# Conditioning vectors as 2048-wide weighted sums, 8 KB weight slots and an opening in eight steps, in a two-layer decoder trunk

## The chip, the cores and the metric

The kernel runs on one core of a Trainium2 chip. The metric is the device time of one execution in microseconds (us), as the median of several runs. The parts of the core are called TensorE (PE in the profile, with PEld for its weight loads), VectorE (DVE), ScalarE (ACT), GpSimd (POOL) and SyncE (SP), which issues most of the DMAs.

## The reference

One sequence of 256 tokens with 2048 features passes through two decoder layers, all in float32. Layer 0 mixes tokens with forgetting attention (FoX, 16 heads of 128), layer 1 with sliding-window grouped attention (SWA, 32 query heads of 64, 4 key/value heads). Each layer then has a gated feed-forward network with a causal convolution (5632 wide). Around each of the four sub-layers stands the conditioning by a vector c:

```python
c_act = jax.nn.silu(c)                              # (1, 2048)
for i in range(DEPTH):                              # 2
    mod = c_act @ ada_w[i] + ada_b[i]               # 2048 x 12288 weights a layer
    sh1, sc1, g1, sh2, sc2, g2 = jnp.split(mod[:, None, :], 6, axis=-1)
    h = x * (1.0 + sc1) + sh1
    y = mixer(h)                                    # fox_attention or swa_attention
    x = layer_norm(DEEPNORM_ALPHA * x + (1.0 + g1) * y, ln_mix_g[i], ln_mix_b[i])
    h = x * (1.0 + sc2) + sh2
    y = conv_ffn(h, ffn_w_up[i], ffn_conv_w[i], ffn_conv_b[i], ffn_w_down[i])
    x = layer_norm(DEEPNORM_ALPHA * x + (1.0 + g2) * y, ln_ffn_g[i], ln_ffn_b[i])
return x
```

The conditioning weights `ada_w` hold 2 x 2048 x 12288 floats, 201 MB of the 600 MB that the kernel reads.

## The kernel before, in words

**Products.** Activations lie transposed in `hH` and `hL`, the rounded value and the remainder of each float, features on the partitions. Weights come in tiles of 128 x 1024 floats (512 KB: two row blocks of 128 by 512 columns) through a pool `wp` of 10 slots of 4 KB a partition. `stream` (L266) issues the DMA on SP, has ScalarE round the tile into `wh` (L272) and VectorE take the remainder into `wl` (L283); the products run two tiles later. Each product is the sum of three: hH by wh, hL by wh, hH by wl. With the weights stationary (`w_mm`, results `ws`) a tile takes 24 products of 256 columns; with the activations stationary (`x_mm`, results `xs`) 12 products of 512 columns. The hidden list `work` holds what is still to be emitted, so the order on every engine is written out by the program.

**Background work.** After each tile `tick` (L367) runs: it adds `ada["rate"]` to a debt and makes one step of the conditioning generator `ada_vector` (L381) for each whole unit. A step before is one DMA of 512 KB (128 rows of c by 1024 columns of `ada_w`) and one VectorE operation (L405) that adds the rows, scaled by the entry of c on their partition, to `acc`. 32 such steps make one of the ten vectors of 2048 that are made this way, `(layer, part)`, and `acc` must still be summed over the partitions: for shift and scale columns by 16 TensorE transposes and ScalarE sums (L469, L473, layer 0) or by VectorE transposes and sums (L447, L451) with a product by `fold` (layer 1); for gate rows (parts 2 and 5) by a split on ScalarE and VectorE and products with ones (the result in `gate`, L421). A gate's bias is put into `acc` by a GpSimd DMA (L393). Rates are set by stage (1.6 a tile at the start of FoX, 0.64 in the first feed-forward). `ada_need` runs the steps that are missing when a vector is wanted.

**Opening.** The first two vectors, shift and scale of layer 0, are needed before any product. `opening` (L565) makes them from `ada_open`, a copy of their weights in tiles of 512 KB, in five steps that cover 1, 1, 2, 2 and 2 pairs of feature blocks (`STEPS`). In a step VectorE adds up the rows (`oacc`, L605), TensorE multiplies some row blocks directly (`products`) and then sums `oacc` over the partitions (`totals`): these are products of one column, in the bank `cps`. Then `cv` (L644) is made, x is transposed (`mod_turn`, L526) and modulated into hH and hL (`mod_pair`, L540, L541). Between these, FoX tiles that need only finished feature blocks are streamed: `plan` lists the pairs (block of 512 columns, pair of feature blocks) by step, each three tiles (query, key, value). Results of a block that is not finished in the opening are copied aside by `keep` (L948) and added later (`sum`, L881).

**Placement.** `place` sets where hH and hL start inside the padded buffer `hpad`: 20 floats in for FoX and the feed-forwards, 56 in for SWA.

Of the kernel before, what the change touches and what calls it, by code (L numbers as in the profile page):

```python
# [17 lines left out]
P = 128  # L18
# [23 lines left out]
def hybrid_trunk(ctx: ExitStack, tc: tile.TileContext, a: dict, out: bass.AP):  # L42
# [13 lines left out]
    def wtile(name="w"):  # L56
        return wp.tile([P, 2, WB], F32, tag="w", name=name)
# [34 lines left out]
    rows0 = ttile("rows0").rearrange("p (a b) -> p a b", b=P)  # L92
    NADA = 6 * KC
    nc.sync.dma_start(rows0[:KC, 0, :], a["c"].rearrange("b (r p) -> (b r) p", p=P))
    adab = a["ada_b"].rearrange("l (r p) -> l r p", p=P)
    nc.sync.dma_start(rows0[:NADA, 1, :], adab[0])

    ones = cst.tile([P, P], F32, name="ones")
# [21 lines left out]
    csil = tp.tile([KC, P], F32, tag="t", name="csil")  # L120
    nc.scalar.activation(csil, rows0[:KC, 0, :], AF.Silu)
    cact = cst.tile([P, KC], F32, name="cact")
    pt = bank()
    nc.tensor.transpose(pt[:, :KC], csil, ident[:KC, :KC])
    nc.vector.tensor_copy(cact, pt[:, :KC])
    cactp = cst.tile([P, KC], F32, name="cactp")
    nc.gpsimd.tensor_scalar_mul(cactp, cact, float(P))
    acol = cst.tile([P, DEPTH, NADA], F32, name="acol")
    pt = bank()
    nc.tensor.transpose(pt[:, :NADA], rows0[:NADA, 1, :], ident[:NADA, :NADA])  # L130
    nc.vector.tensor_copy(acol[:, 0, :], pt[:, :NADA])
# [4 lines left out]
    fold = cst.tile([P, 4, P], F32, name="fold")  # L136
    nc.gpsimd.memset(fold, 0.0)

    NF = 2 * DFF // P
    HR = ROPE_DIM // 2  # L140
# [7 lines left out]
    def columns():  # L148

        r = ttile("rows").rearrange("p (a b) -> p a b", b=P)  # L150
        for l in range(1, DEPTH):
            nc.gpsimd.dma_start(r[:NADA, l, :], adab[l])
        for q, nm in enumerate(("ln_mix_g", "ln_mix_b", "ln_ffn_g", "ln_ffn_b")):
            nc.gpsimd.dma_start(r[q * 32:(q + 1) * 32, 0, :], a[nm].rearrange("l (r p) -> (l r) p", p=P))
        yield
        for l in range(1, DEPTH):
            pt = bank()
            nc.tensor.transpose(pt[:, :NADA], r[:NADA, l, :], ident[:NADA, :NADA])
            yield
            nc.vector.tensor_copy(acol[:, l, :], pt[:, :NADA])  # L160
        pt = bank()
        nc.tensor.transpose(pt[:, :P], r[:, 0, :], ident)
        yield
        nc.vector.tensor_copy(lcol.rearrange("p a b c -> p (a b c)"), pt[:, :P])
        for l in range(DEPTH):
            r = ttile("rows").rearrange("p (a b) -> p a b", b=P)
            for j in range(CW):
                nc.gpsimd.dma_start(r[:NF, j, :], a["ffn_conv_w"][l, j].rearrange("(r p) -> r p", p=P))
            nc.gpsimd.dma_start(r[:NF, CW, :], a["ffn_conv_b"][l].rearrange("(r p) -> r p", p=P))
            for _ in range(4):  # L170
                yield
            pt = bank()
            for j in range(CW + 1):
                nc.tensor.transpose(pt[:, j * NF:(j + 1) * NF], r[:NF, j, :], ident[:NF, :NF])
            yield
            nc.vector.tensor_copy(ccol[:, l].rearrange("p a b -> p (a b)"), pt[:, :(CW + 1) * NF])

    def rotary():

        nc.gpsimd.dma_start(sink, a["swa_sinks"][0].partition_broadcast(P))  # L180
        posr = tp.tile([NT, P], I32, tag="t", name="posr")
        nc.gpsimd.dma_start(posr, a["positions"].rearrange("b (t p) -> (b t) p", p=P))
        yield
        for q in range(4):
            nc.vector.tensor_reduce(fold[:, q, q * 32:(q + 1) * 32], ident.rearrange("p (a i) -> p i a", a=4),
                                    axis=AX.X, op=ALU.add)
        nc.vector.tensor_scalar_mul(nsink, sink, -1.0)
        posf = tp.tile([NT, P], F32, tag="t", name="posf")
        nc.vector.tensor_copy(posf, posr)
        yield  # L190
        pt = bank()
        nc.tensor.transpose(pt[:, :NT], posf, ident[:NT, :NT])
        yield
        posc = cst.tile([P, NT], F32, name="posc")
        nc.vector.tensor_copy(posc, pt[:, :NT])
# [69 lines left out]

    def stream(wsrc, row0, col, ks, use, spare={}):  # L266

        for kc in ks[::2]:
            w = wtile()
            pin(nc.sync.dma_start(w, wsrc[(row0 + kc) // 2, col // WB]), False)  # L270
# [22 lines left out]
    def x_mm(ps, kc, h, l, stat, last, first=0, ts=range(NT)):  # L293

        for t in ts:
            for i in range(2):
# [20 lines left out]
    def w_mm(ps, kc, h, l, last=KC - 1, first=0):  # L317

        for i in range(2):
# [58 lines left out]
    held = []  # L378
    HELD = {}

    def ada_vector(l, v):  # L381
        row = v % 3 == 2
        if (l, v) in HELD and HELD[l, v]:
            q = [cst.tile([P, 512], F32, tag=f"ha{i}", name="ha") for i in range(4)]
            part = lambda c, n: q[c // 512][:, c % 512:c % 512 + n]
            step_ = 512
        else:
            acc = cst.tile([P, D], F32, tag="acc", name="acc")
            part = lambda c, n: acc[:, c:c + n]
            step_ = D // 2  # L390
        if row:

            nc.gpsimd.dma_start(acc, a["ada_b"][l, v * D:(v + 1) * D].partition_broadcast(P))  # L393
            yield
            yield
        for k in range(KC):
            for c in range(0, D, D // 2):
                w = wtile("wa").rearrange("p a f -> p (a f)")
                pin(nc.sync.dma_start(w, a["ada_w"][l, k * P:(k + 1) * P, v * D + c:v * D + c + D // 2]), False)
                for o in range(0, D // 2, step_):  # L400
                    ac, wo = part(c + o, step_), w[:, o:o + step_]
                    if k == 0 and not row:
                        pin(nc.vector.tensor_scalar_mul(ac, wo, cact[:, 0:1]), True)
                    else:
                        pin(nc.vector.scalar_tensor_tensor(ac, wo, (cactp if row else cact)[:, k:k + 1], ac,  # L405
                                                           op0=ALU.mult, op1=ALU.add), True)
                yield
        if row:
            while not ada["gate_free"]:
                yield  # L410
# [11 lines left out]
            gates[l, v] = g  # L422
            return
        ps = []

        def sums():
            ps.append(bank())
            for k in range(KC):
# [53 lines left out]
    def release():  # L482

        for s_, _ in held:
            s_()
# [771 lines left out]
```

## Time and profile before

| What | Value |
|---|---|
| median of 3 runs | 2203.82 us (2203.8 to 2205.1) |
| the profiled execution | 2204.25 us |
| its span, first to last instruction | 2202.5 us |
| granted TensorE clock, mean | 0.995 |
| PE busy, DVE busy, ACT busy, POOL busy | 98%, 82%, 52%, 1% |
| bytes moved by DMA | 602.98 MB, mean 274 GB/s |

The profile is one execution traced by the hardware. Times are microseconds unless marked ns. A line L75 is line 75 of the kernel; since helpers record the products, most of TensorE's work has the line L75 and is told apart by its tiles, written out<-in. Rows of groups give the count, the busy time, the mean duration of one in ns, and after it the idle time of the engine before them with what ended it. Products overlap one another, so their mean duration is longer than their pace. The chain is the work that ended last, followed back from the end: each piece with its start and how long it set the end. Rows of stretches give the stretch, its length and the busy time of each engine with the count of instructions, then the granted TensorE clock, the mean busy share of the 16 DMA engines and the GB/s moved.

### The profile page before, as it was taken

To read this page: it belongs to the slowest core of one execution; us is meant where nothing else is said; L and a number is where in the kernel's file an instruction comes from. 1 tells how busy PE (TensorE), PEld (TensorE's weight loads), DVE (VectorE), ACT (ScalarE), POOL (GpSimd) and SP (SyncE) were. 2 spreads that over 40 slices of the span, in tenths; PEclk is the share of its full clock that TensorE was granted. 3 is DMA by queue.
4 is the path that set the end of the run, shared out by engine and by line. 5 is a ranking of instruction groups with operands and counts; after the bars stand their busy time and mean duration, and the time that the engine had idled before them with its cause. 6 is when DMAs were issued, how large, how long until landed. Compare 5 with 4: busy or idle time off the path is not lost.

```text
span 2202.5 us, 38162 instructions
## 1 busy us (share of the span) xinstructions
PE 2156.7 (98%) x14883; PEld 1968.9 (89%) x14883; DVE 1810.4 (82%) x2487; ACT 1139.3 (52%) x1713; POOL 19.9 (1%) x49
## 2 busy tenths in 40 slices
PE   6999999999999999999999999999999999999997
PEld 6999888789999888999987877789999988999986
DVE  7879999989988989888989888899888655666765
ACT  3435646465565533555534687555555533555541
POOL 0000000000000000000000000000000000000000
PEclk9999999999999999999999999999999999999999
DMA  9999998969968989879888756778878666665662
GB/s 376 376 365 349 357 353 300 326 240 331 348 227 304 329 299 360 278 270 328 307 284 313 236 184 218 257 262 299 282 262 271 186 194 196 192 193 194 194 198 112
DMA packets 166598, 602.98 MB, mean 274 GB/s; under 512 B 18758, under 2 KB 19592, under 8 KB 165904
## 3 DMA queue, kind: packets, MB, share of 16 engines
q1 hardware_dynamic: 165360, 595.85, 78.1%
q0 software_dynamic: 1056, 4.69, 0.7%
q8 instruction: 116, 1.90, 0.3%
q14 instruction: 66, 0.54, 0.1%
HBM read 598.37 MB, written 2.10 MB: 273 GB/s over the span
## 4 chain that ended last, share of the span: by engine, by line
PE 84%; DVE 10%; issue 3%; ACT 2%; DMA 1%; SPq 0%; POOL 0%; DVEq 0%; ACTq 0%; POOLq 0%
PE ws L75 47%; PE xs L75 33%; DVE wl L283 3%; DVE acc L405 3%; DMA wo<-in_ada_open_dram 1%; ACT wh L272 1%; PE cps L75 1%; PE sm L526 1%; PE S L75 1%; DMA w<-in_fox_w_in_dram 1%; PE o L75 1%; DVE pr L734 1%; DVE oacc L605 0%; PE sm L75 0%; PE T L765 0%
## 5 line engine op out<-in xcount | busy, mean ns | idle before, releaser
L272 ACT CAST wh<-w 128x1024 fp32r<-128x1024 f32 x724 | 761.2, 1053 | 788.1 <-PE ws L75 271.2
L75 PE MATMUL ws<-hH,wh 128*128 128x256 f32 x6656 | 1148.9, 277 | 4.4 <-ACT hH L84 1.9
L283 DVE TENSOR_TENSOR wl<-w,wh 128x1024 fp32r<-128x1024 f32 x724 | 882.4, 1221 | 299.7 <-ACT wh L272 288.6
L75 PEld LDWEIGHTS ws<-hH,wh 128*128 128x128 f32 x6656 | 1009.3, 189 | 8.5 <-ACT hH L84 2.1
L75 PE MATMUL ws<-hH,wl 128*128 128x256 f32 x3328 | 916.5, 277 | 4.6 <-DVE wl L283 4.5
L75 PEld LDWEIGHTS ws<-hH,wl 128*128 128x128 f32 x3328 | 626.1, 189 | 6.5 <-DVE wl L283 6.2
L75 PE MATMUL xs<-wh,gT 128*128 128x512 f32 x1376 | 425.3, 389 | 0.0
L75 PEld LDWEIGHTS xs<-wh,gT 128*128 128x128 f32 x1376 | 258.3, 188 | 53.7
L75 PE MATMUL xs<-wl,gT 128*128 128x512 f32 x688 | 267.7, 389 | 0.0
L75 PE MATMUL xs<-wh,hH 128*128 128x512 f32 x704 | 235.8, 402 | 0.0
L405 DVE SCALAR_TENSOR_TENSOR acc<-wa,cact,acc 128x1024 f32<-128x1024 f32 x180 | 228.0, 1278 | 0.0
L405 DVE SCALAR_TENSOR_TENSOR acc<-wa,cactp,acc 128x1024 f32<-128x1024 f32 x128 | 162.5, 1278 | 0.0
L75 PEld LDWEIGHTS xs<-wh,hH 128*128 128x128 f32 x704 | 131.7, 189 | 29.1 <-ACT hH L84 0.3
L75 PEld LDWEIGHTS xs<-wl,gT 128*128 128x128 f32 x688 | 129.1, 188 | 26.5
L75 PE MATMUL xs<-wl,hH 128*128 128x512 f32 x352 | 139.6, 397 | 2.3 <-DVE wl L283 2.3
L1121 ACT ACTIVATE u<-ws,ccol 128x256 f32<-128x256 f32 x176 | 96.8, 562 | 62.1 <-PE ws L75 44.6
L75 PE MATMUL xs<-wh,oT 128*128 128x512 f32 x384 | 125.6, 396 | 0.0
L1122 DVE SCALAR_TENSOR_TENSOR u<-ws,ccol,u 128x255 f32<-128x255 f32 x176 | 82.5, 477 | 13.7 <-ACT u L1121 13.3
L75 PEld LDWEIGHTS xs<-wh,oT 128*128 128x128 f32 x384 | 72.1, 188 | 15.1
L1124 DVE SCALAR_TENSOR_TENSOR u<-ws,ccol,u 128x254 f32<-128x254 f32 x176 | 83.1, 477 | 2.0
L75 PEld LDWEIGHTS xs<-wl,hH 128*128 128x128 f32 x352 | 66.6, 189 | 17.4 <-DVE wl L283 4.1
L75 PE MATMUL xs<-wl,oT 128*128 128x512 f32 x192 | 75.4, 393 | 3.1 <-DVE wl L283 3.1
(231 smaller groups left out, 1290.8 us busy)
## 6 DMA issues: line engine op xcount, KB each, us to landing
w<-in_ffn_w_up_dram SPq DMA_DIRECT2D x352, 512.0 KB, 4.6
wa<-in_ada_w_dram SPq DMA_DIRECT2D x320, 512.0 KB, 5.3
w<-in_ffn_w_down_dram SPq DMA_DIRECT2D x176, 512.0 KB, 4.4
w<-in_fox_w_in_dram SPq DMA_DIRECT2D x96, 512.0 KB, 6.0
wo<-in_ada_open_dram SPq DMA_DIRECT2D x64, 512.0 KB, 8.2
w<-in_swa_w_in_dram SPq DMA_DIRECT2D x40, 512.0 KB, 4.7
w<-in_fox_w_o_dram SPq DMA_DIRECT2D x32, 512.0 KB, 5.4
w<-in_swa_w_o_dram SPq DMA_DIRECT2D x32, 512.0 KB, 4.4
```

What stands on the lines that cost most here:

```text
L75: return nc.tensor.matmul(o, lhsT, rhs, start=start, stop=stop, **kw)
L272: pin(nc.scalar.copy(h, w), False)
L283: pin(nc.vector.tensor_tensor(l, w, f32(h), op=ALU.subtract), behind[0] > 0)
L405: pin(nc.vector.scalar_tensor_tensor(ac, wo, (cactp if row else cact)[:, k:k + 1], ac, op0=ALU.mult, op1=ALU.add), True)
L526: nc.tensor.transpose(o[:, t * P:(t + 1) * P], x[:, t, (k + j) * P:(k + j + 1) * P], ident)
L734: nc.vector.tensor_tensor_reduce(pr[:, b:e].rearrange("p (a k) -> p a k", k=P), S_ps[:, b:e].rearrange("p (a k) -> p a k", k=P), mk, -1.0, ...
L1121: nc.scalar.activation(u, pf, AF.Identity, bias=cw(CW, f), scale=cw(2, f))
L1122: nc.vector.scalar_tensor_tensor(u[:, 1:], pf[:, :S - 1], cw(1, f), u[:, 1:], op0=ALU.mult, op1=ALU.add)
L1124: nc.vector.scalar_tensor_tensor(u[:, 2:], pf[:, :S - 2], cw(0, f), u[:, 2:], op0=ALU.mult, op1=ALU.add)
```

## The change

- `ada_w` is laid out column by column: block (layer, part, k) holds 128 output columns on the partitions with their 2048 weights behind one another. c, passed through SiLU, is kept on all partitions (`cb`, one broadcast DMA of 1 MB and one ScalarE operation). `ada_column` is one DMA of 1 MB and one VectorE `tensor_tensor_reduce` over 2048 elements, which multiplies by `cb`, sums, and starts from the bias: it gives the finished 128 entries. No sum over partitions is left. 32 operations make the opening's two vectors and 160 the other ten.
- A gate row is made from its column: 32 small ScalarE products with the identity matrix make diagonal tiles (rounded value and remainder), which are multiplied by ones; each of these steps refunds half a unit of debt.
- Slots of `wp` become 8 KB a partition, 6 of them. `stream` loads four row blocks (1 MB) at once where it can, and else puts two halves into one slot. All rates are halved.
- The opening has eight steps of one pair of feature blocks each: four `ada_column`s, x, and tiles by a new `plan`. The products of one column are gone. The first step modulates each feature block alone (`mod_one`), and the first block's products are split so that the half that needs the first feature block runs first (`second`). `mod_pair` can make both halves on ScalarE (`on_act`).
- Biases, norm parameters, convolution weights and positions come already laid out as columns, so their transposes go. `place` takes 60 and 32. `ones` moves to a temporary tile, `gp` has 28 buffers for 30, `release` and the held sums go.

```diff
-    wp = ctx.enter_context(tc.tile_pool(name="wp", bufs=10))
+    wp = ctx.enter_context(tc.tile_pool(name="wp", bufs=6))
...
-    gp = ctx.enter_context(tc.tile_pool(name="gp", bufs=30))
+    gp = ctx.enter_context(tc.tile_pool(name="gp", bufs=28))
...
-        return wp.tile([P, 2, WB], F32, tag="w", name=name)
+        return wp.tile([P, UK, WB], F32, tag="w", name=name)
...
+    cb = cst.tile([P, D], F32, name="cb")
+    nc.sync.dma_start(cb, a["c"][0].partition_broadcast(P))
+    acol = cst.tile([P, DEPTH, NADA], F32, name="acol")
+    nc.gpsimd.dma_start(acol, a["ada_b"])
...
+    nc.scalar.activation(cb, cb, AF.Silu)
...
         for kc in ks[::2]:
-            w = wtile()
-            pin(nc.sync.dma_start(w, wsrc[(row0 + kc) // 2, col // WB]), False)
+            g = row0 + kc
+            src = wsrc[g // UK, col // WB]
+            if kc in pend:
+                w = pend[kc]
+            elif g % UK == 0 and kc + 2 in ks:
+                W = wtile()
+                pin(nc.sync.dma_start(W, src), False)
+                w, pend[kc + 2] = W[:, :2], W[:, 2:]
+            else:
+                if halves:
+                    w = halves.pop()
+                else:
+                    W = wtile()
+                    w = W[:, :2]
+                    halves.append(W[:, 2:])
+                pin(nc.sync.dma_start(w, src[:, g % UK:g % UK + 2]), False)
...
+    def ada_column(l, v, k, cv):
+        w = wtile("wa").rearrange("p a f -> p (a f)")
+        pin(nc.sync.dma_start(w, a["ada_w"][l, v * KC + k]), False)
+        return nc.vector.tensor_tensor_reduce(w, w, cb, 1.0, acol[:, l, v * KC + k:v * KC + k + 1],
+                                              ALU.mult, ALU.add, cv[:, k:k + 1])
 
     def ada_vector(l, v):
...
+        cv = cst.tile([P, KC], F32, tag=f"cv{v}", name="cv")
         for k in range(KC):
...
+            pin(ada_column(l, v, k, cv), True)
+            yield
+        if v % 3 < 2:
+            cols[l, v] = cv
+            ada["held"] = v == 4
             return
+        gh, gl = (sp.tile([P, KC], F32R, tag=n, bufs=1, name=n) for n in ("gh", "gl"))
+        split_v(gh, gl, cv)
+        while not ada["gate_free"]:
+            yield
...
+        for j in range(nd + 3):
+            if j > 2:
+                nc.scalar.copy(g[:, (j - 3) * WB:(j - 2) * WB], ps.pop(j - 3))
+            if 1 < j < nd + 2:
+                ps[j - 2] = bank()
+                for i, d in enumerate(diag.pop(j - 2)):
+                    mm(ps[j - 2], onesr, d, start=i == 0, stop=i == 1)
+            if j < nd:
+                diag[j] = [gtile(n).rearrange("p a b -> p (a b)") for n in ("dh", "dl")]
+                for d, c in zip(diag[j], (gh, gl)):
+                    for q in range(WB // P):
+                        k = j * (WB // P) + q
+                        nc.scalar.mul(d[:, q * P:(q + 1) * P], ident, f32(c)[:, k:k + 1])
+            ada["debt"] += 0.5
+            yield
+        gates[l, v] = g
...
-    place(20)
+    place(60)
...
+    def mod_one(G, B, k):
+        ps, t = bank()[:, :S], ttile()[:, :S]
+        for j in range(NT):
+            nc.tensor.transpose(ps[:, j * P:(j + 1) * P], x[:, j, k * P:(k + 1) * P], ident)
+        g, b = G[:, k:k + 1], B[:, k:k + 1]
+        nc.scalar.activation(hH[:, k, :], ps, AF.Identity, bias=b, scale=g)
+        nc.scalar.activation(t, ps, AF.Identity, bias=b, scale=g)
+        nc.vector.tensor_tensor(hL[:, k, :], t, f32(hH[:, k, :]), op=ALU.subtract)
...
         todos = [[(*it, part) for it in items for part in range(3)] for items in plan]
-        for s_, todo in enumerate(todos):
+        for s_ in range(KC // 2):
+            k0, todo = 2 * s_, todos[s_]
             n = len(todo)
...
+            for i in range(4):
+                ada_column(0, 1 - i % 2, k0 + i // 2, cols[0, 1 - i % 2])
+                if i == 1:
+                    c = slice(k0 * P, (k0 + 2) * P)
                     nc.sync.dma_start(x[:, :, c], a["x"][0][:, c].rearrange("(t p) d -> p t d", p=P))
...
+                while todo and n - len(todo) < (i + 1) * n // 4:
                     proj(*todo.pop(0))
...
+                if s_ == 0 and i > 0:
+                    if i < 3:
+                        proj(*todos[1].pop(0))
+                    if i % 2:
+                        mod_one(cols[0, 1], cols[0, 0], i // 2)
+            if s_ > 0:
+                for _ in range(min(2, len(todos[s_ + 1]))):
+                    proj(*todos[s_ + 1].pop(0))
+                mod_pair(cols[0, 1], cols[0, 0], k0, mod_turn(k0), False, True, True)
+        prep()
+        then(lambda: ada.update(rate=0.8))
+        for it in todos[KC // 2]:
+            proj(*it)
...
-        plan = [[], [(2, 0), (1, 0)], [(1, 1), (3, 0), (3, 1)], [(3, 2), (3, 3), (0, 0), (0, 1)],
-                [(0, 2), (0, 3), (0, 4), (0, 5)], [(0, 6), (0, 7)]]
+        plan = [[], [(2, 0), (1, 0)], [(1, 1)], [(1, 2), (3, 0), (3, 1)], [(3, 2), (3, 3)], [(3, 4), (0, 0), (0, 1)],
+                [(0, 2), (0, 3), (0, 4)], [(0, 5), (0, 6)], [(0, 7)]]
...
-        for blk, rate in zip((0, 2, 1, 3), (1.6, 1.6, 1.5, 1.4)):
+        for blk, rate in zip((0, 2, 1, 3), (0.8, 0.8, 0.75, 0.7)):
...
-        place(20 if v else 56)
+        place(60 if v else 32)
...
+    out["ada_w"] = a["ada_w"].transpose(0, 2, 1).reshape(DEPTH, 6 * KC, P, D)
+    out["ada_b"] = a["ada_b"].reshape(DEPTH, 6 * KC, P).transpose(2, 0, 1)
```

More of the change, by code (lines that the diff above doesn't have):

```diff
@@ L119, in hybrid_trunk @@
     x = cst.tile([P, NT, D], F32, name="x")
[L120 to L131, printed above, removed]
+    nc.scalar.activation(cb, cb, AF.Silu)
+    for v in (1, 4):
+        c1 = acol[:, :, v * KC:(v + 2) * KC]
+        nc.gpsimd.tensor_scalar_add(c1, c1, 1.0)
     onesr = cst.tile([P, P], F32R, name="onesr")
     nc.vector.tensor_copy(onesr, ones)
[L136 to L140, printed above, removed]
     lcol = cst.tile([P, 4, DEPTH, KC], F32, name="lcol")
@@ L161, in columns @@
[L161 to L176, printed above, removed]
+        nc.gpsimd.dma_start(lcol, a["ln_col"])
@@ L178, in rotary @@
+        nc.gpsimd.dma_start(ccol, a["conv_col"])
+        yield
     def rotary():
         nc.gpsimd.dma_start(sink, a["swa_sinks"][0].partition_broadcast(P))
[L181 to L193, printed above, removed]
+        posr = cst.tile([P, NT], I32, name="posr")
+        nc.gpsimd.dma_start(posr, a["positions"])
+        for _ in range(3):
+            yield
+        pin(nc.vector.tensor_scalar_mul(nsink, sink, -1.0))
         posc = cst.tile([P, NT], F32, name="posc")
-        nc.vector.tensor_copy(posc, pt[:, :NT])
+        pin(nc.vector.tensor_copy(posc, posr))
```

287 lines of the change are left out of this document (64 added, 223 removed).

## The prediction

> **What bounds the kernel now.** I read the page first, then stretches by stage, then the chain of each stage.
>
> ```profile
> span 2202.5 us, 38162 instructions
> PE 2156.7 (98%) x14883; PEld 1968.9 (89%) x14883; DVE 1810.4 (82%) x2487; ACT 1139.3 (52%) x1713; POOL 19.9 (1%) x49
> PE 84%; DVE 10%; issue 3%; ACT 2%; DMA 1%; SPq 0%; POOL 0%; DVEq 0%; ACTq 0%; POOLq 0%
> ...
> 0.00:20.00 20.00, 11.05 (x46) 9.97 (x46) 10.57 (x20) 6.80 (x11) 4.10 (x21) 1.00 0.89 317
> 20.00:60.00 40.00, 32.25 (x187) 29.89 (x187) 34.86 (x44) 17.44 (x24) 0.00 (x0) 0.87 1.03 409
> 60.00:160.00 100.00, 99.43 (x716) 93.12 (x715) 84.34 (x83) 40.97 (x49) 2.52 (x5) 0.97 0.97 368
> 203.00:367.00 164.00, 158.01 (x1102) 143.94 (x1101) 152.78 (x228) 98.11 (x209) 0.57 (x1) 1.00 0.93 337
> 500.00:1100.00 600.00, 599.33 (x4644) 574.01 (x4644) 537.73 (x661) 309.91 (x403) 0.59 (x1) 1.00 0.88 308
> 1200.00:1410.00 210.00, 206.61 (x1152) 160.57 (x1153) 175.32 (x426) 146.68 (x335) 0.55 (x1) 1.00 0.65 210
> ```
>
> TensorE ends last for 84% of the span. In the feed-forward (500 to 1100) only less TensorE work can gain anything. The room is in three places: the opening, where the DMA engines are full (0.89 to 1.03 of their time) and TensorE starts late; FoX from 203 to 367, where VectorE is busy 152.78 of 164 us; and SWA after 1200.
>
> Busy time doesn't tell useful products from others, so I count weight tiles. The first two rows give the products with results ws and xs up to 203 us; then come their pace in the chain, the one-column products of a step's end, and the start of the first ws:
>
> ```profile
> 0.00:203.00 203.00, 111.94 (x866) 109.17 (x867) 2.75 (x4) 9.34 (x16) 0.96 0.97 369
> 0.00:203.00 203.00, 47.46 (x180) 33.62 (x180) 0.00 (x0) 4.38 (x8) 0.96 0.97 369
> ...
> 84.51 5.52 PE ws L75 x48
> 98.38 2.83 PE xs L75 x12
> 74.52 3.46 PE cps L75 x32
> ...
> L75 PEld LDWEIGHTS ws<-hH,wh x6656: 186/188/335, 21.0 to 2081.6; 128*128 128x128 f32 x196
> ```
>
> 866/24 + 180/12 = 51 tiles are done at 203 us. A tile costs (2 x 2.76 + 2.83)/3 = 2.78 us, so they are 142 us of useful work, and 61 of the first 203 us are lost: 21 before the first product, the rest at step ends.
>
> **The change, part by part.** *One conditioning operation.* Two operations of 1024 become one of 2048.
>
> ```profile
> L405 DVE SCALAR_TENSOR_TENSOR acc<-wa,cact,acc 128x1024 f32<-128x1024 f32 x180 | 228.0, 1278 | 0.0
> L734 DVE CUSTOM_DVE_ANT_0 pr<-S,mask,nsink 128x256 f32<-128x256 f32 x32 | 15.4, 480 | 0.0
> L734 DVE CUSTOM_DVE_ANT_0 pr<-S,mask,nsink 128x128 f32<-128x128 f32 x32 | 11.0, 344 | 0.0
> L734 DVE DVE_READ_ACCUMULATOR2_ANT nm<- 128x1 f32 x96 | 8.0, 84 | 0.0
> ...
> 200.94 2.39 DVE acc L405 x2
> ```
>
> The pair costs 2.39 us. The nearest rows for the new operation are the masked minima of attention, also `tensor_tensor_reduce`: (480 - 344)/128 = 1.06 ns an element, so 2048 take 480 + 1792 x 1.06 = 2384 ns. Back to back, operations overlap by about 83 ns (1278 against 2.39/2), which gives 2.30 us, or 2.38 if the read of the accumulator (84 ns) adds. I take 2.34: as good as even. These minima read one source from PSUM; L405 reads two f32 sources from SBUF at full rate, but writes no accumulator. No row has both, so the upper bound is open; one at half rate would be 2 x 2.3 = 4.6 us.
>
> [...]
>
> *The opening.* What each step must bring, in order on SP's queue: four columns of 1.05 MB, x 0.26, tiles of 0.524 each by `plan` (two of a step are pulled ahead), and first `cb`, 1.05. I run them at the stretches' rates: 6.3 MB by 20 us, 22.7 by 60, then 0.368 MB/us. Each pair of blocks is modulated some 4.5 us after its step's bytes land:
>
> ```profile
> L540 ACT ACTIVATE t<-sm,B,G 128x256 f32<-128x256 f32 x18 | 9.8, 561 | 0.1
> L84 ACT CAST hH<-t 128x512 fp32r<-128x512 f32 x25 | 15.5, 620 | 12.5 <-DVE t L541 12.2
> L85 DVE TENSOR_TENSOR hH<-t,hH 128x512 fp32r<-128x512 f32 x25 | 17.1, 686 | 0.5 <-ACT hH L84 0.4
> ```
>
> (2.34 for the last column, two of 0.56, 0.62 and 0.69, less what passes while the step's last tiles land.) The steps end at 6.6, 14.2, 20.2, 29.4, 37.0, 46.2, 55.4 and 61.4 MB, so at 21, 39, 54, 78, 99, 124, 149 and 165 us, and the pairs are ready at 25, 43.7, 58.5, 82.7, 103.5, 128.5, 153.5 and 169.5. TensorE then goes: 6 tiles to 42 (the first half-products run from about 14, when `cb` and two columns, 3.2 MB, have landed by 10 and 2.34 and two of 0.56 us have passed, which saves 2.7; 3 us are put down for the half clock behind waits, since the granted clock was 0.87 in 20 to 60); 3 tiles to 52.5; waits for the third pair; 9 tiles to 84; 6 to 101; waits 2.5; 9 to 129; 9 to 154.5; 6 to 171.6; the last 3 to **180 us**. That includes 0.45 us of transposes a step. The one-column products (144, gone) are no part of it. So 51 tiles are done at 180 instead of 203: **-23 us**. Bounds: TensorE never waiting after the second pair gives 43.7 + 45 x 2.78 + 4 = 173 (-30); each of the seven later ends losing 3.5 us, the length of the group at 74.52, instead of the 10 us of waits above gives 194 (-9). DMA is the cover that keeps TensorE from more: it stays full until 165.
>
> *The rest of FoX.* 45 tiles remain either way. Before, 55 operations of 1024 ran in 203 to 367 (66.44 us, first row below). After, the rates summed over those tiles give 36.8 steps, and with the refunds some 32 columns: 32 x 2.34 = 75 us. Gone is one gate's split (4 x 0.69). VectorE must do 75 - 66.4 - 2.7 = 5.9 us more in the stage where it is busy 93%: **+6 us** (0 if TensorE hides it, +12 if a long operation delays `wl` each time).
>
> ```profile
> 203.00:367.00 164.00, 66.44 (x55) 1.00 0.93 337
> ...
> L85 DVE TENSOR_TENSOR al<-acc,ah 128x512 fp32r<-128x512 f32 x16 | 10.8, 686 | 0.3 <-ACT ah L84 0.3
> L447 DVE STREAM_TRANSPOSE acc<-acc 128x512 f32<-128x512 f32 x16 | 10.9, 698 | 0.1
> L451 DVE TENSOR_REDUCE red<-acc 128x32 f32<-128x1024 f32 x8 | 9.6, 1203 | 0.0
> L469 PE MATMUL sm<-ident,acc 128*128 128x128 f32 x32 | 4.5, 272 | 0.0
> L75 PE MATMUL sm<-red,fold 128*128 128x16 f32 x32 | 3.8, 253 | 0.0
> L748 ACT ACTIVATE pr<-pr,ss 128x128 f32<-128x128 f32 x16 | 6.4, 402 | 4.2 <-DVE ss L746 4.1
> ...
> 1199.90 1.32 issue
> 1201.23 0.02 POOLq L393
> ```
>
> *Gates on ScalarE.* 32 products of 128x128, at most 402 ns each (L748), 13 us a gate instead of 4 casts. FoX's gate falls into a few tiles around 360, where each `wh` queues behind eight of them; two tiles of lead cover 5.6 us: **+2** (0 to +6). The other three gates go out at a lower rate: 0.
>
> *Sums over partitions.* 32 transposes (4.5 us) and 32 `fold` products (3.8) leave TensorE; where it is the only bound (the feed-forward, three of four vectors) that counts: **-2** (0 to -8).
>
> *The norm before SWA.* The chain waits 1.32 us for GpSimd, whose queue holds the gate's bias DMA (L393): **-1.3**.
>
> *SWA.* A vector's transposes and sums, 4 x 0.70 + 2 x 1.20, and one split, 2.7, leave VectorE, which is busy 175 of 210 us: **-3** (0 to -8).
>
> *Slots, queue, place.* Six slots of 1 MB hold 6 MB where ten held 5; a column blocks its slot until VectorE is done, as before: 0 (a stall of SP's queue would show in the opening, bound above). For `place` I add up the tile sizes: hH stands 112 bytes behind the weights (mod 256) before and after, 0 in SWA: 0, with the pace as rival.
>
> **Sum:** -23 + 6 + 2 - 2 - 1.3 - 3 = -21.3. The profiled execution took 2204.25 us (0.4 above the median of the runs), so **2183 us**.
>
> **Rivals.** *Given back.* FoX ends when the queue has brought its bytes: 130 MB by 367 before (the stretches' rates times their lengths, with 15 in 160 to 203). After: tiles 50.3, 64 columns 67.1, x and cb 3.1, and the same 9 read ahead, 129.5. At the same mean rate the first two terms are 0 and the time is 2200. For it: 0.93 to 1.03 busy engines. Against: VectorE's 93%, and 409 GB/s once.
>
> *More.* Opening at its bound, VectorE no hindrance: -30 - 2 - 1.3 - 8 = 2163.
>
> *Slower: the sum runs at half rate*, 4.6 us. Opening: 4 x 4.6 + 6.4 tiles x 1.14 + 0.7 = 26 us a step against 22: +28. FoX: 32 x 2.2 = 70; out projection 17 x 2.2 = 37; feed-forward 64 x 2.2 less its 62 us of room, 79; SWA 30. About 2430 us. It decides from about 2.65 us on, where 21 us are spread over some 69 operations on the path. The minima's slope speaks against it, their PSUM source leaves it open. [...]
>
> *Slower: another pace of the products.* Paces differ with the operands' places:
>
> ```profile
> 1108.14 71.97 PE xs L75 x317
> 869.72 73.48 PE ws L75 x648
> ```
>
> 236 ns with hH at 112 bytes (98.38 above), 227 with gT at 0, 113.4 for ws. If my sum of sizes is off and ws pays the same 3.5%, 9984 products cost 40 us more: 2223.
>
> **How the numbers follow.** The forecast 0.50 (2172 to 2194), given back 0.18, more 0.13, half rate 0.08, another pace 0.04, a stall of the six slots 0.07. 2162 to 2206 leaves out the last three and a little below. A difference under 0.2% (4.4 us) can't be told from none here: faster takes the forecast, more and half of given back, and a little of the rest, 0.74; same 0.12; slower 0.14.
>
> **What would show it.** Right: 51 tiles near 180 us, first ws near 14; no cps; the new operation near 2.38 us; FoX's last value tiles near 350; the rest shifted by a constant, ws still 113 ns. Wrong: the new operation over 2.65 us; VectorE's `wl` releasing TensorE in the feed-forward; the opening's last column far behind 165 us.

## The result and the profile after

The changed kernel takes 2193.45 us against 2205.1 us for the kernel before on the same chip: ratio 0.9944 [0.9928, 0.9960]; by the medians 11.7 us less. One of its five runs, at 7584.84 us, lies far outside the other four (2191.84 to 2195.05) and is left out of the ratio. The forecast was 2183, 21 less: the direction held, and a little under half of the gain is missing. The time lies just inside the forecast's stretch of 2172 to 2194.

From the page of the changed kernel: span, engines and shares of the chain; then the rows of the new operation.

```profile
span 2193.0 us, 36104 instructions
PE 2133.5 (97%) x14662; PEld 1941.2 (89%) x14662; DVE 1763.9 (80%) x2410; ACT 1160.8 (53%) x1770; POOL 15.6 (1%) x35
PE 86%; DVE 8%; issue 2%; ACT 2%; DMA 2%; POOL 0%; DVEq 0%; SPq 0%; ACTq 0%; POOLq 0%
```
```profile
L355 DVE CUSTOM_DVE_ANT_0 wa<-wa,cb,acol 128x2048 f32<-128x2048 f32 x192 | 450.0, 2345 | 7.3 <-DMA wa<-in_ada_w_dram 6.8
L355 DVE DVE_READ_ACCUMULATOR2_ANT cv<- 128x1 f32 x192 | 15.9, 83 | 0.0
```

TensorE has lost 23 us of busy time and the span only 9.5: part of the saved work came back as waiting. Where, the windows by stage show (columns as before: busy time and instructions of PE, PEld, DVE, ACT, POOL, then granted clock, DMA share, GB/s), with the useful products of the opening last:

```profile
0.00:20.00 20.00, 4.38 (x16) 3.43 (x16) 9.13 (x9) 10.31 (x14) 9.83 (x25) 1.00 0.92 352
20.00:60.00 40.00, 33.62 (x180) 28.76 (x181) 36.03 (x32) 17.52 (x25) 0.00 (x0) 0.91 1.02 418
60.00:160.00 100.00, 100.00 (x729) 93.25 (x728) 85.64 (x78) 49.93 (x61) 0.00 (x0) 1.00 1.01 404
178.40:342.90 164.50, 152.73 (x1102) 140.63 (x1100) 154.04 (x222) 87.54 (x154) 0.57 (x2) 1.00 0.90 340
500.00:1100.00 600.00, 600.00 (x4640) 574.39 (x4639) 532.10 (x648) 316.88 (x430) 0.00 (x0) 1.00 0.85 317
```
```profile
0.00:178.40 178.40, 103.41 (x816) 101.03 (x817) 1.38 (x2) 7.99 (x15) 0.98 0.99 396
0.00:178.40 178.40, 55.81 (x204) 38.90 (x204) 0.00 (x0) 3.94 (x7) 0.98 0.99 396
```

The last two rows are the products into ws and xs: 816/24 + 204/12 = 51 tiles, done at 178.4 us, where the kernel before had the same number at 203. From 60 to 160 us TensorE doesn't wait at all. In the feed-forward it is busy all the time too, as it was before.

Counting weight tiles (6144 columns each) along the trace in the same way gives the time at which every stage ends, and so what each term of the prediction was worth. Each column is one profiled execution, and these two differ by 9.2 us at the end where the medians differ by 11.7. Nine kernels with the new opening, at the same place of hH, reach tile 51 between 177.0 and 179.2 us; from there on, kernels that don't differ up to a point reach it in the same time to within 0.6 us.

| up to | before, us | after, us | this stage, us | predicted |
|---|---|---|---|---|
| tile 51, end of the opening | 202.8 | 178.4 | -24.4 | -23 |
| tile 96, end of FoX's input projections | 361.4 | 342.9 | +5.9 | +6 |
| tile 100 | 374.7 | 370.7 | **+14.5** | **+2** (gates) |
| tile 128, end of FoX's output projection | 463.8 | 460.4 | +0.6 | 0 |
| first `u` of the feed-forward | 494.8 | 494.2 | +2.8 | 0 |
| last residual before SWA | 1198.1 | 1193.6 | -3.9 | -2 (sums) |
| last residual of SWA | 1461.3 | 1451.4 | -5.4 | -4.3 (norm, SWA) |
| last residual of all | 2190.9 | 2181.7 | +0.7 | 0 |

One stage, four tiles long, holds the miss. Its two rows, before and after:

```profile
361.40:374.70 13.30, 13.30 (x65) 11.15 (x64) 11.77 (x14) 7.38 (x12) 0.00 (x0) 1.00 0.87 293
```
```profile
342.90:370.70 27.80, 23.69 (x93) 17.37 (x92) 13.04 (x32) 26.66 (x75) 0.00 (x0) 0.82 0.38 135
```

ScalarE went from 7.38 of 13.3 us to 26.66 of 27.8, TensorE fell to the half clock (granted 0.50) from 353.2 to 363.4 us, 0.82 in the mean of the stage, and the DMA engines were busy for 0.38 of the time, since SP's queue waited for slots, 12.9 us of it for one `wl`. The chain of the changed kernel there:

```profile
345.86 0.94 ACT wh L246
346.80 0.70 ACT pr L605 x2
347.50 1.17 ACT dh L387 x4
348.67 1.17 ACT dl L387 x4
349.85 1.17 ACT dh L387 x4
351.02 1.17 ACT dl L387 x4
352.18 0.36 ACT pT L624
352.55 0.89 ACT pr L595 x4
353.44 0.94 ACT wh L246
```

Two kinds of work stand between one cast of weights (`wh`) and the next: the gate's products (dh, dl, the change's own), and the softmax of attention (pr, pT), which in the kernel before was over by then.

### The profile page after: what moved, and what is told of

Its sections match the earlier page's. It is cut to its first block, busy times and chain, and to the rows that moved or that the text cites. A ratio compares the mean times of both kernels' runs of the same rounds, so it can differ in the third digit from the quotient of the medians.

```text
span 2193.0 us, 36104 instructions
## 1 busy us (share of the span) xinstructions
PE 2133.5 (97%) x14662; PEld 1941.2 (89%) x14662; DVE 1763.9 (80%) x2410; ACT 1160.8 (53%) x1770; POOL 15.6 (1%) x35
## 2 busy tenths in 40 slices
DMA packets 89671, 599.65 MB, mean 273 GB/s; under 512 B 10016, under 2 KB 12224, under 8 KB 21024
## 4 chain that ended last, share of the span: by engine, by line
PE 86%; DVE 8%; issue 2%; ACT 2%; DMA 2%; POOL 0%; DVEq 0%; SPq 0%; ACTq 0%; POOLq 0%
PE ws L75 48%; PE xs L75 34%; DVE wa L355 3%; DVE wl L257 2%; DMA wa<-in_ada_w_dram 1%; PE o L75 1%; PE S L75 1%; PE T L622 1%; DMA w<-in_fox_w_in_dram 1%; PE sm L428 1%; ACT wh L246 0%; DVE x L521 0%; DVE t L519 0%; PE sm L75 0%; PE spin L75 0%
## 5 line engine op out<-in xcount | busy, mean ns | idle before, releaser
L355 DVE CUSTOM_DVE_ANT_0 wa<-wa,cb,acol 128x2048 f32<-128x2048 f32 x192 | 450.0, 2345 | 7.3 <-DMA wa<-in_ada_w_dram 6.8
L75 PEld LDWEIGHTS xs<-wh,hH 128*128 128x128 f32 x704 | 133.0, 191 | 33.8 <-ACT wh L246 4.7
L595 ACT ACTIVATE pr<-pr,nm 128x128 f32<-128x128 f32 x96 | 43.1, 451 | 21.9 <-DVE nm L591 21.6
```

The costliest lines, as they stand in the source:

```text
L75: return nc.tensor.matmul(o, lhsT, rhs, start=start, stop=stop, **kw)
L355: return nc.vector.tensor_tensor_reduce(w, w, cb, 1.0, acol[:, l, v * KC + k:v * KC + k + 1], ALU.mult, ALU.add, cv[:, k:k + 1])
L595: nc.scalar.activation(pr[:, b:e], pr[:, b:e], AF.Exp, bias=nm[:, r:r + 1], scale=-1.0, accum_out=ss[:, r:r + 1])
```

## Experiments

### The gate's products: moved, doubled, paced

`gate_dve` and `gate_pool` make the same 32 products as eight operations of 128x512 on VectorE or GpSimd; `gate_twice` makes them twice for layer 0's first gate; `gate_norefund` drops the refund that makes the conditioning sums go on faster while a gate is made.

```
-    for q in range(WB // P):
-        k = j * (WB // P) + q
-        nc.scalar.mul(d[:, q * P:(q + 1) * P], ident, f32(c)[:, k:k + 1])
+    nc.vector.tensor_tensor(d (p, q, f), ident broadcast over q, c broadcast over f, op=ALU.mult)   # gate_dve
+    nc.gpsimd.tensor_tensor(... the same ...)                                                       # gate_pool
```
```
+    if (l, v) == (0, 2): nc.scalar.mul(...)      # gate_twice: the same product once more
...
-    ada["debt"] += 0.5                            # gate_norefund
```

> The 32 diagonal products of each gate go from ScalarE to VectorE, as 8 products of 128x512, some 0.6 us each, 4.8 us a gate. Theory (ScalarE burst): ScalarE is freed of 9.5 us in the chain, VectorE gets 4.8 us in a stage where it is 93% busy: 2182 to 2188. Rival (open attention): 2193 to 2198.

> The 32 diagonal products of each gate go from ScalarE to GpSimd, as 8 products of 128x512. Theory (ScalarE burst: between tiles 96 and 100 the weight casts queue behind the 32 products, 27.8 us for four tiles instead of 13.3): tiles 96 to 100 take 13 to 15 us and the median falls by 10 to 14 us, to 2180 to 2184. Rival (attention of the last blocks, which the tiles covered before, now lies open, whatever ScalarE does for the gate): tiles 96 to 100 stay above 24 us and the median at 2190 to 2195.

> Each diagonal product of layer 0's first gate is made twice: 32 more ScalarE operations of 0.29 us each. Theory (ScalarE burst): 9 to 10 us more between tiles 96 and 100, 2202 to 2206. Rival (open attention): under 3 us more.

> The refund of half a unit of debt at each step of a gate is taken out, so the 32 products spread over twice as many tiles. Theory (ScalarE burst): about half of the 14.5 us lost between tiles 96 and 100 comes back, 2185 to 2189; a vector that is late behind it could cost some of it. Rival (open attention): 2192 to 2195.

| kernel | time, us | ratio to before | tiles 96 to 100, us |
|---|---|---|---|
| after | 2193.45 | 0.9944 [0.9928, 0.9960] | 27.8 |
| `gate_dve` | 2185.32 | 0.9910 [0.9894, 0.9927] | 20.3 |
| `gate_pool` | 2189.27 | 0.9927 [0.9913, 0.9942] | 20.1 |
| `gate_twice` | 2201.68 | 0.9983 [0.9974, 0.9992] | 37.1 |
| `gate_norefund` | 2201.40 | 0.9986 [0.9977, 0.9995] | 24.8 |

A second dose costs 9.3 us in the stage, and taking the dose away gives back 7.5: the products stand on the path. But 7 us over the 13.3 of before remain with either engine. `gate_dve` came out as its theory said, and `gate_twice` in the stage; in `gate_pool` the four tiles lie between theory and rival. `gate_norefund` was a miss: the stage gains 3 us, but the last sum of vector (0,4) then starts at 465.9 us instead of 452.1 and stands in the chain ahead of the feed-forward, whose first `u` comes 40.5 us after tile 128 instead of 33.8. The refund keeps a deadline. At this `u` the kernel is only 1.8 us behind; 3.4 us more are lost in SWA (261.2 us instead of 257.8).

`gate_pool` ends 4 us above `gate_dve`, for a reason that none of the theories had. The norm before SWA, instruction by instruction (start, length, and in brackets the idle time before it with what ended it): five rows of `gate_pool`, then the normalisation in the changed kernel.

```profile
1186.97 0.15 DVE L532 TENSOR_SCALAR mv<-mv 128x1 f32<-128x1 f32 x1
1187.21 0.55 POOL L533 TENSOR_TENSOR rs<-mv,mhalf 128x1 f32<-128x1 f32 x1 [2.18 <-DVE mv L532]
1187.72 1.04 POOL L385 TENSOR_TENSOR dh<-ident,gh 128x512 fp32r<-128x512 f32 x1
1187.79 4.80 DVE L545 TENSOR_SCALAR x<-x,mv,rs 128x512 f32<-128x512 f32 x4 [0.66 <-POOL rs L533]
1191.09 1.22 POOL L385 TENSOR_TENSOR dl<-ident,gl 128x512 fp32r<-128x512 f32 x1
```
```profile
1196.85 1.92 DVE L544 TENSOR_SCALAR x<-x,mv,rs 128x512 f32<-128x512 f32 x4 [0.67 <-POOL rs L532]
```

`rs` itself isn't late: it starts 0.09 us after VectorE's `mv`. But then GpSimd makes four of the gate's products, of 1.04 to 1.22 us, and beside them four normalising operations of VectorE take 4.80 us instead of 1.92. TensorE waits for them and runs at half clock from 1194.0 to 1197.5 us (the granted clock is 0.97 in the mean of 1190 to 1250); at SWA's eighth tile `gate_pool` is 4.3 us further behind `gate_dve` than at the last residual. The 4.80 us beside GpSimd's products and the 1.92 us without them agree with the two engines hindering each other; by what mechanism, no run here shows.

### Where the attention stands

Counting the weight tiles that TensorE issues ahead of each attention product shows a second move, which the prediction had passed over. The output projection asks for block 1's results from tile 98 on. In the kernel before, block 1's last four `o` are issued at tiles 95, 96, 97 and 98; in the changed one the first `T` stands at 96, the other three at 98, and the `o` at 98 to 99.25, all at once. The cause is `plan`: the opening now takes two pairs of rows more, (1, 2) and (3, 4), so block 3, streamed last, has 9 tiles left instead of 12, and block 1's attention has three tiles fewer to hide behind. `plan_swap` gives block 1 the five pairs and block 3 the three; `plan_gate` adds this to `gate_dve`.

```
-  plan = [[], [(2, 0), (1, 0)], [(1, 1)], [(1, 2), (3, 0), (3, 1)], [(3, 2), (3, 3)], [(3, 4), (0, 0), (0, 1)], ...
+  plan = [[], [(2, 0), (3, 0)], [(3, 1)], [(3, 2), (1, 0), (1, 1)], [(1, 2), (1, 3)], [(1, 4), (0, 0), (0, 1)], ...
```

> In the opening's list of products the numbers of FoX blocks 1 and 3 are exchanged: block 1 gets five pairs of rows in the opening and block 3 three, so that block 3, streamed last, has 15 tiles left instead of 9, and block 1's attention, which the out-projection asks for from tile 98 on, is issued beside tiles 86 to 95 of the program instead of 91 to 99. Same work, ScalarE still multiplies the gate's products. Theory (two causes side by side: the gate's burst on ScalarE, and the attention that stands three tiles later because six tiles went from the blocks to the opening): tiles 96 to 100 take 20 to 21 us instead of 27.8, time 2185 to 2188. Rival, the burst alone is the cause and the place of the attention costs nothing: 27 to 28 us, 2192 to 2195. Rival, the two cost only where they meet: 14 to 15 us, 2179 to 2182.

> The exchanged blocks and the gate's products on VectorE together. Theory (two causes): tiles 96 to 100 in 14 to 15 us, near the 13.3 of the kernel before; time 2178 to 2181, six below the kernel with the gate on VectorE alone (2185.3). Rival, what was left there is ScalarE's own load (gate copies, casts of weights, softmax), wherever the attention stands: 19 to 20 us, 2184 to 2187.

The four tiles in `gate_dve`, `plan_swap` and `plan_gate`:

```profile
343.80:364.10 20.30, 18.82 (x94) 15.28 (x93) 17.11 (x40) 18.16 (x45) 0.00 (x0) 1.00 0.62 220
```
```profile
347.30:362.10 14.80, 13.58 (x58) 10.36 (x57) 6.65 (x8) 14.80 (x38) 0.00 (x0) 1.00 0.51 183
```
```profile
347.40:360.20 12.80, 12.80 (x58) 10.52 (x57) 12.75 (x17) 8.17 (x12) 0.00 (x0) 1.00 0.74 270
```

In these four tiles, with neither move 12.8 us; the burst alone (`plan_swap`) 14.8, +2.0; the late attention alone (`gate_dve`) 20.3, +7.5; both 27.8, +15.0. The two cost 5.5 us more together than one by one; in the chain above both queue on ScalarE between the casts of the same weights. The window of four tiles flatters the exchange, though, as the attention now costs time ahead of tile 96 (51 to 96 take 168.8 us in `plan_swap`, 164.5 in the changed kernel). From tile 51 to the first `u` the same four take 305.4 us (neither), 307.5 (burst alone), 307.5 (late attention alone) and 315.8 (both): each alone costs about 2 us, and their meeting 6.2. That fits the rival that the two cost only where they meet better than the theory of two causes side by side.

The times didn't follow: `plan_swap` 2193.68 (0.9946 [0.9934, 0.9959]) and `plan_gate` 2192.52 (0.9939 [0.9926, 0.9953]), where the theories had 2185 to 2188 and 2178 to 2181. In `plan_swap` 8.2 us are still there at the first `u` (486.0 us against 494.2), and SWA, with 262.9 us instead of 257.8, takes 5.1 of them. In `plan_gate`, held against `gate_dve`, two things took the gain. First, up to the first `u` little of it arrives: `gate_dve` gets there at 484.5 us, `plan_gate` at 484.1, although it took 7.5 us less for the four tiles. It is 1.7 us behind at tile 51, where the programs differ only in names (kernels with this opening lie at 177.0 to 179.2), then takes 1.9 us longer to tile 96 and 3.5 from tile 100 to `u`. VectorE is busy 285.64 of 307.5 us from tile 51 to `u` in one and 285.23 of 305.4 in the other: with 93% of that stretch full, the likely reason is that freeing ScalarE for four tiles moves the wait to VectorE; no run tests it. Second, SWA takes 264.9 us in `plan_gate` and 258.0 in `gate_dve`, with the same work. The exchange had shifted the counter that paces the conditioning sums by 0.3 (from 0.45 to 0.15 at the first feed-forward: six tiles more pass at 0.7 a tile and six fewer at 0.75), and so the place of each sum among SWA's instructions. `plan_phase` puts this back:

```
         ada_need(l, v + 1)
+        if (l, v) == (0, 3):
+            ada["debt"] += 0.3
```

> The kernel with exchanged blocks and gate products on VectorE, with one constant more: 0.3 is added to the counter that paces the conditioning sums, once, when the first feed-forward begins, so that from there on each sum is issued at the place that it has in the kernel with the gate on VectorE alone (the exchange had shifted the counter by 0.3, and SWA then took 265 us instead of 258). Theory (the shift of the sums against SWA's attention costs the 7 us): SWA back at 257 to 259 us, time 2184 to 2187. Rival (something else of the exchange costs it): SWA stays at 264 to 265 us, 2191 to 2194.

2185.83 us (0.9903 [0.9886, 0.9919]); SWA takes 258.0 us. The stage's window in `plan_gate` and `plan_phase`, and pieces of `plan_gate`'s chain at the second of the two spots where it falls behind `gate_dve` (2.0 us at SWA's tiles 26 to 28, 4.5 at tiles 42 to 48):

```profile
1200.00:1410.00 210.00, 206.10 (x1134) 160.51 (x1133) 172.99 (x416) 138.57 (x319) 0.00 (x0) 0.98 0.59 215
```
```profile
1200.00:1410.00 210.00, 208.47 (x1163) 163.25 (x1162) 179.45 (x423) 141.05 (x322) 0.00 (x0) 1.00 0.63 227
```
```profile
1356.96 2.26 DVE wa L355
...
1359.91 1.14 DVE wl L257
...
1362.28 0.49 ACT pr L955
1362.77 0.95 ACT wh L246
...
1366.98 4.54 PE xs L75 x12
```

Sums of 2.26 us stand in the chain ahead of a `wl` and of attention's work on VectorE and ScalarE. TensorE, which had waited, then runs at half clock from 1367.0 to 1370.4 us, as it does at the first spot from 1278.4 to 1281.7: twelve products take 4.54 us where 2.78 is usual, and the granted clock is 0.96 in the mean of 1265 to 1303 and of 1337 to 1375, 0.98 in the stage. In `plan_phase` the chain from 1350 to 1370 us has TensorE's work alone. So the place of the same sums, moved by 0.3 of a step, is worth 7 us.

### Half of the sums in FoX

```
-    return nc.vector.tensor_tensor_reduce(w, w, cb, 1.0, acol...
+    n = D // 2 if (l, v) in ((0, 3), (0, 2)) else D
+    return nc.vector.tensor_tensor_reduce(w[:, :n], w[:, :n], cb[:, :n], 1.0, acol...
```

> The weighted sums of the vectors (0,3) and (0,2) run over the first 1024 of their 2048 products; their DMAs stay whole. This leaves out half of these two vectors' sums. VectorE saves 32 x 1.1 = 35 us from 180 to 340 us. Theory (VectorE bounds the rest of FoX): tiles 51 to 96 take 164.5 us now and then 135 to 145; the end of the kernel gains the same less what the gate burst and the output projection take. Rival (the DMA queue bounds it): 160 to 165 us, no gain.

This kernel leaves out half of two vectors' sums and serves as a probe alone. 2184.12 us (0.9899 [0.9884, 0.9913]). Tiles 51 to 96 take 157.7 us instead of 164.5. The window of the stretch in `half_sum`:

```profile
177.50:335.00 157.50, 151.19 (x1101) 140.26 (x1100) 122.95 (x223) 88.44 (x157) 0.56 (x2) 1.00 0.92 355
```

VectorE falls from 154 to 123 us and the stage gains only 6.8: with a fifth of its load gone TensorE is the floor, busy 151.19 of 157.5 us. In the chain of this stretch the sums have 3% instead of 24%, and the products into ws and xs 66% instead of 22%. So the sums are worth those 6.8 us here. That the +5.9 against the kernel before is the same excess is a reading, not tested by itself: there VectorE's operations of L405 hold 18% of the chain too, but the stage, with 158.6 us, lies near the floor. The expected 135 to 145 was a miss.

### The one-column products of the opening

They are gone in the change, and the prediction gave them no price. `cps_free` issues 20 at the end of seven steps on data that is there from the start, `cps_dep` the same on the tile that the step's last sum writes, `cps_same` ten. In TensorE's order the groups stand behind tiles 4, 5, 14, 16, 29, 31 and 36 in `cps_free` and `cps_same`, and behind 4, 8, 16, 23, 31, 40 and 47 in `cps_dep`.

```
+        def one_col(w):
+            ps = bank("cps")
+            for c in range(20):            # cps_same: 10
+                mm(ps[:, c:c + 1], w[:, c % KC * P:(c % KC + 1) * P], ident[:, 0:1], start=True, stop=True)
...
             if s_ > 0:
+                one_col(cb)                # cps_dep: the tile of the step's last sum
```

> 20 one-column products are put back at the end of each of seven opening steps, 140 in all, on data that are there from the start, so that TensorE waits for nothing. Theory (they held TensorE for their own length, 0.11 us each): tile 51 comes at 178.4 + 15 = 193 to 196 us. Rival (they cost by waiting for VectorE's sums, or the opening is held by the DMA queue): 178 to 182.

> The same 140 one-column products, now on the tile that the step's last weighted sum has written, so TensorE waits in order for VectorE as it did before. Theory (length alone): as with free data, tile 51 at 193 to 196. Rival (the wait costs more than the length): tile 51 at 200 us or later, that is 8 to 20 us behind the free variant.

> Ten one-column products at the end of each of seven opening steps, on data that is there from the start: 140 passes on TensorE, as many as the kernel before had. Theory (their cost is in proportion to their number: passes and lowered clock): half of the 39.6 us of twenty, tile 51 at 196 to 200, time 2211 to 2216. Rival, the clock is lowered only from some density on: tile 51 at 184 to 189, 2199 to 2204.

Each product is recorded as two passes, so `cps_free` and `cps_dep` had 280, twice the 144 of the kernel before, and `cps_same` 140. The passes of `cps_same` and TensorE's window from 60 to 160 us; then the same two rows of `cps_free`, and two groups of its chain:

```profile
L75 PE MATMUL cps<-ident,cb 128*128 128x1 f32 x140 | 16.0, 246 | 0.0
```
```profile
60.00:160.00 100.00, 99.88 (x711) 93.78 (x710) 74.28 (x67) 41.98 (x51) 0.00 (x0) 0.95 0.93 359
```
```profile
L75 PE MATMUL cps<-ident,cb 128*128 128x1 f32 x280 | 37.2, 268 | 0.0
```
```profile
60.00:160.00 100.00, 100.00 (x673) 94.61 (x673) 62.96 (x57) 38.71 (x49) 0.00 (x0) 0.88 0.80 308
```
```profile
37.34 4.37 PE cps L75 x40
...
134.99 6.09 PE cps L75 x40
```

Tile 51 comes at 194.8 us with 140 passes (+16.4; 2208.4 us, 1.0019 [1.0010, 1.0028]), at 218.0 with 280 (+39.6; 2236.36, 1.0136 [1.0121, 1.0151]), and at 224.7 in `cps_dep` (2245.18, 1.0172 [1.0156, 1.0187]). 40 passes take 4.37 us at 37.34, 0.109 each (in the kernel before 32 take 3.46 us, 0.108 each, at a granted clock of 1.00), and 6.09 us at 134.99; the granted clock from 60 to 160 us is 1.00, 0.95 and 0.88 with none, 140 and 280. So their cost grows faster than their number. `cps_free` came later than both theory and rival had it, and `cps_same` lies between the two.

`cps_dep` doesn't measure a wait for fresh sums: TensorE is busy all the time from 60 us on, and what it waited for ahead of these passes is ScalarE's `wh`, 3.5 us. Its 6.7 us over `cps_free` come with another order, and neither of its expectations was met.

At the dose of the kernel before, the passes thus account for some 16 of the opening's 24.4 us, though that kernel spread them otherwise over its steps; in its own chain they hold 13.9 us. In its trace TensorE also stands idle ahead of them, 5.3 us for VectorE's row sums and 3.5 us for their weights. That this is the rest of the gain is a reading that no run tests.

### The place of the modulated input

```
-    place(60)                      -        place(60 if v else 32)
+    place(20)                      +        place(20 if v else 56)
```

> hH starts 20 and 56 floats in, as in the kernel before, instead of 60 and 32; with the new tile sizes that is 208 and 96 bytes (mod 256) behind the weights instead of 112 and 0. Theory (the paces of the products follow that distance, and the change of place only keeps it): the pace of ws moves from 113 ns, by up to 4 ns in either direction, 40 us at most over 9984 products; the time moves with it. Rival (the distance does nothing): pace 113 ns and a time within 2 us.

2246.2 us (1.0175 [1.0158, 1.0192]). The longest pieces of ws in the first feed-forward's chain, in the changed kernel and in `place_old`:

```profile
499.94 122.97 PE ws L75 x1083
```
```profile
499.96 132.15 PE ws L75 x1109
```

113.5 ns a product against 119.2, more than the 4 ns and the 40 us put as the most. All the code of the change is there, only hH starts 20 floats in instead of 60 (in SWA 56 instead of 32), and the kernel is 53 us slower for it. So the retuned `place` wins nothing over before; left alone, it would have cost the gain four times over. The 112 and 208 bytes are sums of tile sizes, and taking them mod 256 was the author's assumption; whether the distance to the weights counts or hH's own address, one move doesn't tell.

## Why the prediction was right in direction and short in size

**The new operation.** Taken as 2.34 us, measured 2.345, at a pace of 2.26 to 2.27 in the chain. The half-rate rival is refuted: two f32 sources in SBUF, an accumulator read of 83 ns, and 2.345 us instead of 4.6.

**The opening.** -24.4 against -23, and the inner times hold: tile 18 at 84.8 (predicted 84), 24 at 102.0 (101), 33 at 127.4 (129), 42 at 152.9 (154.5), 51 at 178.4 (180). Two steps were off. The first 30 us won nothing: the chain waits for column bytes and then for tiles, and though the first product starts at 15.5 us (predicted 14, before 21), the second tile ends at 31.3 us, in the kernel before at 30.2. And tile 9 comes at 59.2, predicted 52.5: its `wl` stands behind four sums on VectorE, and TensorE then runs at half clock (granted 0.50 from 52.8 to 59.6 us).

```profile
13.27 15.12 DMA wa<-in_ada_w_dram
...
28.40 12.72 DMA w<-in_fox_w_in_dram
...
44.56 2.26 DVE wa L355
...
53.99 1.15 DVE wl L257
...
55.18 4.61 PE xs L75 x10
```

The sum had TensorE wait here for the third pair until 58.5, and that pair was ready at 58.7. So the late tiles fill the time that was put down as a wait: that this step came out right is in part luck. Behind it the queue ran at 404 GB/s where 368 was assumed, with about half as many packets (89671 in the kernel, 166598 before), and the 2.5 us of waiting behind tile 24 didn't come; that the fewer packets are the reason isn't shown. The named cover was wrong: from 60 to 160 the DMA engines are full (1.01), but TensorE is busy 100 of 100 us, and when the one-column products slow it the DMA share falls (0.93, 0.80). And the source of the gain was not spelled out: for some 16 us the one-column products.

**The rest of FoX.** +6 predicted, +5.9 measured. VectorE's busy time rose by 5.1 us (148.91 to 154.04), and `half_sum` shows that its sums hold 6.8 us of the stage: the mechanism fits, though the +5.9 is not traced sum by sum.

**Gates on ScalarE: the step that failed.** +2 (0 to +6) was forecast, +14.5 came. The burst was placed well, and alone it has the price of the sum: 2.0 us (`plan_swap` against `plan_gate`). What failed is the sentence that 45 tiles remain either way. That is true of their number and not of their order: six tiles had moved out of blocks 1 and 3, block 1's attention was left with 9 tiles of cover instead of 12, and its softmax met the burst on the same engine. In the four tiles the late attention alone costs 7.5 us and the meeting 5.5 more; up to the first `u` the burst and the late attention cost about 2 us each and the meeting 6.2. The other terms missed by -1.4, -0.1, -1.9 and -1.1 us, and by +0.6, +2.8 and +0.7 where nothing was put down. Together that is -0.4, so it is partly luck that this one step is the whole miss.

**Given back.** This rival had the right size in part (2193 lies between it, 2200, and the forecast, nearer to it), but not its mechanism: the DMA share falls to 0.38 where the time is lost, so the queue doesn't hold the end of FoX.

**Norm, sums, SWA.** The sums' -2 measured -3.9 through the feed-forward. The +2.8 ahead of it was not foreseen, and its cause stays open: the last sum of (0,4) ends at 454.4 us, before tile 128, but TensorE is at half clock (granted 0.50) from 465.8 to 469.2 and waits 2.4 us for hH at 481.5. The norm's wait of 1.32 us was a misreading: it is idle time of GpSimd, whose `rs` starts 0.09 us after VectorE's `mv`. VectorE waited only 0.46 us, for the first `rs`. Rows of the kernel before, then the chain of the changed one:

```profile
1199.94 0.16 DVE L667 SCALAR_TENSOR_TENSOR rs<-mv,rs 128x1 f32<-128x1 f32 x1 [0.46 <-POOL rs L674]
1201.03 0.15 DVE L673 TENSOR_SCALAR mv<-mv 128x1 f32<-128x1 f32 x1
1201.27 0.55 POOL L674 TENSOR_TENSOR rs<-mv,mhalf 128x1 f32<-128x1 f32 x1 [1.36 <-DVE mv L673]
```
```profile
1196.03 0.17 DVE mv L531
...
1196.27 0.56 POOL rs L532
```

So from the last residual's first operation to the normalisation 3.78 - 3.29 = 0.5 us are won, not 1.3.

SWA with the norm gave -5.4 for -4.3. VectorE's busy time in the stage fell by 13 us (226.61 to 213.61), but how much of the gain that is stays open: the place of the sums alone moves SWA by 7 us, and the kernel before took 263.2 us, nearer to the badly placed 264.9 than to 257.8.

**Another pace.** Its condition (a wrong sum of sizes) didn't arise: ws takes 113.5 ns, as before. Its price, put at 40 us, is 53 in `place_old`.

The best versions here are `gate_dve` (2185.32 us, 0.9910) and `plan_phase` (2185.83 us, 0.9903), which can't be told apart, both below the kernels before and after.

## What to carry to other kernels

When a change moves work from one stage into an earlier one, ask what was hidden behind the work that left: a count that stays the same can hide an order that doesn't. A burst on an engine that is half idle can be cheap alone (here 2.0 us in four tiles) and dear where another latecomer queues on the same engine (5.5 us more), so the two are tested together and apart. And where a pacing counter spreads background work, any edit ahead shifts its phase for the rest of the program; a difference of 7 us far from the edit may be no more than that.

## What the runs showed of the hardware

- One-column f32 products are recorded as two passes each (`cps_same`: 140 passes for 70 products), of 0.108 us at a granted clock of 1.00 (kernel before: 32 in 3.46 us), and lower the granted clock: over 60 to 160 us it is 1.00 with none (changed kernel), 0.95 with 140 passes in the opening (`cps_same`), 0.88 with 280 (`cps_free`).
- The pace of a 256-column product depends on where its moving operand lies: 113.5 ns with hH 60 floats in (changed kernel), 119.2 with it 20 floats in (`place_old`).
- Four 128x512 normalisations on VectorE take 1.92 us in the changed kernel and 4.80 in `gate_pool`, beside GpSimd products of 1.04 to 1.22 us.
